# The second mixer's attention, run one head pair behind itself

## The chip, the cores and the metric

One core of a Trainium2 chip runs the whole program. The metric is the time of one execution in device microseconds. TensorE (PE in the profile, PEld for its weight loads), VectorE (DVE), ScalarE (ACT), GpSimd (POOL) and SyncE (SP) each work through a queue of their own, in order, and wait for one another at semaphores.

## What is computed

Two groups of tokens (512 and 256, width 1024) go through the same two-layer encoder trunk. Each layer is a half-weighted SwiGLU block, a mixer, and another such block. The change lies in the mixer of the second layer, an attention of 16 heads of 64 in which each token sees a neighbourhood on a grid 64 wide, with a bias by relative position:

```python
def neighbourhood_attn(q, k, v, rpb):
    ...
    def one_row(args):
        ...
        bias = rpb[:, dr][:, :, dc]
        s = jnp.einsum('bchd,bacjhd->bhcaj', q_row, k_win).astype(jnp.float32) * (HEAD_DIM ** -0.5)
        s = s + jnp.transpose(bias, (0, 2, 1, 3)).astype(jnp.float32)[None]
        p = jax.nn.softmax(s.reshape(B, NA_HEADS, GRID_W, kh * NA_KW), axis=-1)
        p = p.reshape(B, NA_HEADS, GRID_W, kh, NA_KW).astype(v.dtype)
        return jnp.einsum('bhcaj,bacjhd->bchd', p, v_win)

def mixer_c(h, w_qkv, rpb, w_out):
    qkv = (h @ w_qkv).reshape(B, L, 3, NA_HEADS, HEAD_DIM)
    o = neighbourhood_attn(qkv[:, :, 0], qkv[:, :, 1], qkv[:, :, 2], rpb)
    return o @ w_out
```

## The kernel before

Activations lie transposed, with the width over the partitions. Every product of 32-bit numbers is done as three matmuls of a high and a low part (`hi*hi + hi*lo + lo*hi`), so each operand is first split: ScalarE rounds the high part (lines 111 and 193), VectorE subtracts it (112 and 194).

`mixer1` makes queries and keys for one pair of heads at a time (`qk`), and values for four heads at a time (`v_heads`). These projections are the steady work of TensorE; they write `ps_mm`. Beside them runs the attention, a Python generator. `mm3` counts an estimated time for every matmul, and `tick` resumes a generator when this clock has passed the gap that it yielded (`GAPS1`). So the order of TensorE's queue is fixed when the program is built; the other queues are ordered by the compiler's scheduler. A generator that waits for a list to fill yields 0.5 until it is full.

The steps of one head pair `pr`:

- `scores`: three portions `s` of two blocks for both heads, 12 matmuls each into two banks of the pool `aux` (four PSUM banks, used in turn). `finish_rows` then takes, on VectorE, bias and minimum (line 878), on ScalarE the exponential with its sum (883), on VectorE the reciprocal (890) and the scaling of four sets of rows (892). The result lies in the tiles `p{parity}{block}{head}`, two sets by the parity of `pr`.
- `turn`: four transposes on TensorE (line 141) into one `aux` bank, split into `th` and `tl`. Three of them for each head.
- `values_a`, `values_b`: value matmuls of one head into two `aux` banks, which `put` adds up into the output `o` (lines 1255 and 1256).

Before, a pair's three portions come first, then the transposes and values of its first head, then those of the second. The next pair's bias is made on GpSimd (1172) from tables that SyncE loads (1165). `parts` writes the queries and keys of a pair when the pair ahead has been scored.

`mixer_out` is the output projection. It begins with the chunks of six pairs (`early`): each output is split into `oh` and `ol`, the projections go on while the last attention runs, and line 826 adds the old activations.

Of the kernel before, what the change touches and what calls it, by code (L numbers as in the profile page):

```python
# [10 lines left out]
F32R = mybir.dt.float32r  # L11
# [5 lines left out]
P = 128  # L17
D = 1024
KD = D // P
FF = 2816  # L20
NPAIR = FF // (2 * P)
TA, TB = 512, 256
T = TA + TB
# [20 lines left out]
WTOTAL = 12 * D * FF + 8 * EARLY * P * D + D * 1792 + 2 * D * D + D * 3072 + D * 512  # L44
GAP0 = 4.6
SGU = (8.0, 3.0, 4.0)
GAPS1 = (2.4, 3.0, 0.7, 2.0, 0.8)


class Trunk:  # L50
# [1096 lines left out]
    def mixer1(self):  # L1147
        nc = self.nc
        mp = self.mixer_open("m1")
# [11 lines left out]
        def bias(h):  # L1161
            ba = mp.tile([P, 8, 32], F32, tag="ba", name="ba", bufs=2)
            bb = mp.tile([P, 4, 48], F32, tag="bb", name="bb", bufs=2)
            for t, tab in zip((ba, bb), self.tabs):
                nc.sync.dma_start(t.rearrange("p a c -> p (a c)"), tab[h])
            ba, bb = ba.rearrange("p a c -> p c a"), bb.rearrange("p a c -> p c a")
            res, o = [], 0
            for src, k0, k1 in ((ba, 8, 32), (ba, 0, 32), (ba, 0, 24), (bb, 8, 48), (bb, 0, 40)):
                n = (k1 - k0) * src.shape[2]
                a = mp.tile([P, n], F32, tag=f"add{len(res)}", name="add", bufs=2)  # L1170
                v = lambda t: t.rearrange("p (c a) -> p c a", c=k1 - k0)
                nc.gpsimd.tensor_tensor(out=v(a), in0=v(mb[:, o : o + n]), in1=src[:, k0:k1, :], op=ALU.subtract)
                o += n
                res.append(a)
            return res
# [6 lines left out]
        for par in (0, 1):  # L1182
            for j, (_, c0, c1, s0) in enumerate(SCORE):
                for h in (0, 1):
                    t = pp[par, j, h] = mp.tile([P, 256], F32, tag=f"p{par}{j}{h}", name=f"p{par}{j}{h}")
# [5 lines left out]
        def scores(pr, s):  # L1191
            q, k, st = heads[pr][:3]
            ps = [self.psum(self.aux, "aux") for _ in (0, 1)]
            ps_list, outs, sums = [], [], []
            for i in (0, 1):
                j = 2 * s + i
                qc, c0, c1, s0 = SCORE[j]
                n = c1 - c0
                o = i * (160 if s == 2 else 256)
                dst = [t[:, o : o + n] for t in ps]  # L1200
                rows = lambda h: slice(h * 64, h * 64 + 64)
                self.halves3(
                    dst, [tuple(t[rows(h), qc : qc + P] for t in q) for h in (0, 1)],
                    [tuple(t[rows(h), c0:c1] for t in k) for h in (0, 1)],
                )
                ps_list += dst
                outs += [pp[pr % 2, j, h][:, s0 : s0 + n] for h in (0, 1)]
                sums += [adds[2 * pr + h][(0, 1, 1, 2, 3, 4)[j]] for h in (0, 1)]
            self.finish_rows(mp, st, 4 * s, ps_list, outs, sums, [3e38] * 4)

        def split_t(src):
            pt = self.psum(self.aux, "aux")
            for i, s in enumerate(src):
                self.tpose(pt[:, i * P : (i + 1) * P], s)
            th = mp.tile([P, 512], F32R, tag="th", name="th", bufs=4)
            tl = mp.tile([P, 512], F32R, tag="tl", name="tl", bufs=4)
            self.split(th, tl, pt)
            return th, tl

# [7 lines left out]
        def turn(pr, t, h):  # L1227
            return split_t([pp[pr % 2, j, h][:, c] for j, c in TURN[t]])

        def values_a(po, vt, hv, ii, tt):  # L1230
            for i in (2 * ii, 2 * ii + 1):
                c = (i % 2) * 256
                for t in tt:
                    if i == 0:
                        dst = po.rearrange("p (j q) -> p j q", j=4)[:, 0::3, :]
                        rhs = t[:, c : c + 256].rearrange("p (j q) -> p j q", j=2)
                    else:
                        dst = po[:, (i - 1) * P : (i + 1) * P]
                        rhs = t[:, c : c + 256]
                    self.mmul(  # L1240
                        dst, vt[i][:, hv, :], rhs, i == 0 and t is tt[0], i == 3 and t is tt[1], skip_group_check=True
                    )

        def values_b(po, vt, hv, tt):
            for b in range(2):
                for t in tt:
                    self.mmul(
                        po[:, 0:256], vt[4 + b][:, hv, :], t[:, b * 256 : b * 256 + 256],
                        b == 0 and t is tt[0], b == 1 and t is tt[1],
                    )  # L1250

        def put(pr, h, po, c0, c1):
            n = c1 - c0
            tb = mp.tile([P, 512], F32, tag="tb", name="tb")[0:64, :n]
            nc.scalar.copy(tb, po[64:128, :n])
            nc.vector.tensor_tensor(
                out=ot[pr][h * 64 : h * 64 + 64, c0:c1], in0=po[0:64, :n], in1=tb, op=ALU.add
            )

        heads, scored, adds = [], [], {}  # L1260

        def attention():
            for pr in range(8):
                while pr >= len(heads):
                    yield 0.5
                q, k, st, vt, hv = heads[pr]
                for s in range(3):
                    scores(pr, s)
                    if s < 2:
                        yield GAPS1[0]  # L1270
                scored.append(pr)
                for h in (0, 1):
                    adds.pop(2 * pr + h)
                    if 2 * pr + h + 2 < 16:
                        adds[2 * pr + h + 2] = bias(2 * pr + h + 2)
                yield GAPS1[1]
                tt = {}
                for h in (0, 1):
                    for t in range(3):
                        tt[t, h] = turn(pr, t, h)  # L1280
                        yield GAPS1[2]
                    while len(vt) < 6:
                        yield 0.5
                    yield GAPS1[3]
                    po = self.psum(self.aux, "aux")
                    for t in (0, 1):
                        values_a(po, vt, hv + h, t, tt[t, h])
                        yield GAPS1[4]
                    put(pr, h, po, 0, TA)
                    po = self.psum(self.aux, "aux")  # L1290
                    values_b(po, vt, hv + h, tt[2, h])
                    put(pr, h, po, TA, T)
                    yield GAPS1[4]

        adds[0], adds[1] = bias(0), bias(1)
        att = self.spawn(attention())
        def parts(pr, t, vt, hv):

# [26 lines left out]
        def v_heads(qd, vt):  # L1325
            wv = sum((self.unit("l1_w_qkv", 4 * i, 4, 2048 + qd * 256, 256) for i in (0, 1)), [])
            for i in range(6):
                ps = self.psum()
                for k in range(KD):
                    self.mm3(  # L1330
                        ps[:, 0:256], self.xcols(k, i * P, (i + 1) * P), wv[k],
                        k == 0, k == KD - 1,
                    )
                pv = ps[:, 0:256].rearrange("p (h d) -> p h d", h=4)
                v = mp.tile([P, 4, P], F32R, tag="vt", name="vt", bufs=9)
                r = self.ry[:, i : i + 1]
                nc.scalar.activation(v[:, :, 0:64], pv, AF.Copy, scale=r)
                nc.vector.scalar_tensor_tensor(
                    out=v[:, :, 64:128], in0=pv, scalar=r, in1=v[:, :, 0:64].bitcast(F32),
                    op0=ALU.mult, op1=ALU.subtract,  # L1340
                )
                vt.append(v)

        last = None
        for qd in range(4):
            for i in (0, 1):
                if last:
                    self.drain(last)
                new = qk(2 * qd + i)
                if i == 0:  # L1350
                    vt = []
                last = self.spawn(parts(2 * qd + i, new, vt, 2 * i))
                if i == 0:
                    v_heads(qd, vt)
        self.drain(last)
        self.mixer_out("l1_w_out", [ot[k] for k in range(KD)], att, True)


# [182 lines left out]
```

## Time and profile before

| | |
|---|---|
| median of 3 runs | 2680.07 us (2679.75 to 2681.55) |
| profiled execution | 2677.91 us, span 2676.1 us |
| mean granted clock of TensorE | 0.988 |
| second mixer, scores of pair 0 to values of pair 7 | about 1809 to 2104 us of the span |
| TensorE busy from 1860 to 2060 | 36.4 to 38.6 us of each 40 |

Lines of the profile name engine, source line, operation and tiles (out<-in). A wait is idle time of an engine just before an instruction, put down to what released it. Matmuls overlap: one of 0.28 us may start 0.11 us after the one before it. The gap between starts tells more than the busy time.

### The profile page before, as it was taken

Reading aid. Unit: us, or ns where it says so; the run is one execution under the profiler, and the core shown is the slowest. Engines: PE = TensorE matmul, PEld = TensorE weight load, DVE = VectorE, ACT = ScalarE, POOL = GpSimd, SP = SyncE. Lnnn points to the kernel's source line nnn. Section 1 sums busy time; section 2 is a strip of 40 time slices with the busy share of each in tenths; the row PEclk is TensorE's granted clock in tenths of the full one; section 3 lists DMA queues with packets and bytes.
Section 4 is the critical chain, followed back from the end, with each engine's and each line's share of the span. In section 5 each row is a group of like instructions: output and inputs, shape, how many; then the busy total and the mean of one; then the engine's idle time right before and its main releaser. Section 6 shows DMA issues by size and latency. Waiting matters only on the chain.

```text
span 2676.1 us, 41168 instructions
## 1 busy us (share of the span) xinstructions
PE 2583.9 (97%) x15150; PEld 2510.0 (94%) x15150; DVE 2263.4 (85%) x4748; ACT 1372.1 (51%) x2847; POOL 80.5 (3%) x124
## 2 busy tenths in 40 slices
PE   6999999999999999999999999999999989999997
PEld 6999999977889999999999999988888989999997
DVE  8988889789769988898998898886666599888886
ACT  7545444555756544455654454454545365454443
POOL 0000000000100000000000000011111100000000
PEclk9999999999999999999999999989999999999999
DMA  5333222421223222222322222232211322222221
GB/s 164 116 86 98 78 65 72 148 72 38 86 75 91 79 68 79 64 79 79 95 79 71 72 74 69 79 116 62 62 55 43 99 87 79 79 64 79 65 86 55
DMA packets 82746, 214.80 MB, mean 80 GB/s; under 512 B 19952, under 2 KB 32752, under 8 KB 82544
## 3 DMA queue, kind: packets, MB, share of 16 engines
q1 hardware_dynamic: 82400, 212.14, 25.8%
q8 instruction: 119, 1.95, 0.3%
q14 instruction: 83, 0.68, 0.1%
q10 hardware_dynamic: 144, 0.03, 0.0%
HBM read 202.70 MB, written 15.07 MB: 81 GB/s over the span
## 4 chain that ended last, share of the span: by engine, by line
PE 88%; DVE 6%; ACT 4%; issue 1%; DMA 0%; SPq 0%; DVEq 0%; ACTq 0%
PE ps_mm L137 56%; PE ps_aux L137 31%; ACT p L883 2%; DVE p L892 1%; PE ps_aux L141 1%; DVE wlo L112 1%; DVE xl L710 1%; ACT whi L111 0%; DVE p L878 0%; DMA raw<-in_w 0%; ACT xh L709 0%; DVE x L632 0%; DVE x L677 0%; DVE ol L194 0%; ACT sq L216 0%
## 5 line engine op out<-in xcount | busy, mean ns | idle before, releaser
L111 ACT CAST whi<-s 128x512 fp32r<-128x512 f32 x496 | 302.0, 620 | 377.6 <-DVE s L580 134.1
L111 ACT CAST whi<-raw 128x512 fp32r<-128x512 f32 x512 | 311.7, 618 | 283.6 <-PE ps_mm L137 127.8
L112 DVE TENSOR_TENSOR wlo<-s,whi 128x512 fp32r<-128x512 f32 x496 | 335.0, 685 | 71.6 <-ACT whi L111 71.2
L112 DVE TENSOR_TENSOR wlo<-raw,whi 128x512 fp32r<-128x512 f32 x494 | 335.8, 685 | 39.1 <-ACT whi L111 34.5
L137 PE MATMUL ps_aux<-dt,whi 128*128 128x384 f32 x864 | 221.6, 338 | 0.0
L137 PE MATMUL ps_mm<-db,whi 128*128 128x384 f32 x864 | 221.6, 338 | 0.0
L137 PEld LDWEIGHTS ps_mm<-db,whi 128*128 128x128 f32 x864 | 156.8, 188 | 0.0
L137 PEld LDWEIGHTS ps_aux<-dt,whi 128*128 128x128 f32 x864 | 156.8, 188 | 0.0
L137 PE MATMUL ps_mm<-xh,whi 128*128 128x512 f32 (+1 forms) x416 | 147.7, 355 | 3.0 <-ACT xh L709 3.0
L137 PE MATMUL ps_mm<-db,wlo 128*128 128x384 f32 x432 | 146.0, 338 | 0.0
L137 PE MATMUL ps_aux<-dt,wlo 128*128 128x384 f32 x432 | 146.0, 338 | 0.0
L137 PE MATMUL ps_mm<-xl,whi 128*128 128x512 f32 (+1 forms) x416 | 142.7, 343 | 1.1 <-DVE xl L710 1.1
L137 PE MATMUL ps_mm<-xh,wlo 128*128 128x512 f32 (+1 forms) x416 | 142.2, 342 | 0.0
L472 DVE TENSOR_TENSOR u<-ps_aux,u 128x384 f32<-128x384 f32 x176 | 96.9, 551 | 5.2 <-PE ps_aux L137 3.9
L580 DVE TENSOR_TENSOR s<-raw,raw 128x512 f32<-128x512 f32 x124 | 83.3, 685 | 20.8 <-DMA raw<-in_w 20.8
L467 ACT COPY u<-ps_mm 128x384 f32<-128x384 f32 x176 | 83.5, 474 | 33.4 <-PE ps_mm L137 33.2
L137 PE MATMUL ps_aux<-dh,whi 128*128 128x384 f32 x384 | 98.5, 338 | 0.6 <-DVE x L677 0.6
L580 DVE TENSOR_TENSOR s<-raw 128x512 f32<-128x512 f32 x124 | 84.8, 685 | 16.8 <-DMA raw<-in_w 16.8
L883 ACT ACTIVATE p<-p,st 128x256 f32<-128x256 f32 (+3 forms) x144 | 69.2, 481 | 54.2 <-DVE st L878 54.1
L632 DVE TENSOR_TENSOR x<-ps_aux,x 128x384 f32<-128x384 f32 x160 | 86.3, 551 | 11.1 <-PE ps_aux L137 11.0
L137 PE MATMUL ps_mm<-oh,whi 128*128 128x384 f32 x256 | 89.6, 350 | 5.1 <-DVE x L861 4.0
L632 DVE TENSOR_TENSOR x<-ps_mm,x 128x384 f32<-128x384 f32 x160 | 86.8, 550 | 6.1 <-PE ps_mm L137 5.9
(427 smaller groups left out, 8087.2 us busy)
## 6 DMA issues: line engine op xcount, KB each, us to landing
raw<-in_w SPq DMA_DIRECT2D x342, 512.0 KB, 3.7
xdm<-x SPq DMA_DIRECT2D x16, 384.0 KB, 2.4
x<-in_x SPq DMA_DIRECT2D x16, 192.0 KB, 5.6
x<-xdm SPq DMA_DIRECT2D x8, 384.0 KB, 3.5
xold<-xdm SPq DMA_DIRECT2D x8, 384.0 KB, 3.1
out_y<-y SPq DMA_DIRECT2D x8, 384.0 KB, 2.5
tab<-skew SPq DMA_DIRECT2D x8, 256.0 KB, 4.4
raw<-in_w SPq DMA_DIRECT2D x8, 256.0 KB, 2.6
```

The lines of the kernel that those rows point to most:

```text
L111: nc.scalar.copy(hi, src)
L112: (eng or nc.gpsimd).tensor_tensor(out=lo, in0=src, in1=hi.bitcast(F32), op=ALU.subtract)
L137: self.nc.tensor.matmul(out, lhsT=lhsT, rhs=rhs, start=start, stop=stop, **kw)
L141: self.nc.tensor.transpose(out, src, self.ident)
L467: nc.scalar.copy(e[n, out], bank[key, n])
L472: nc.vector.tensor_tensor(out=t, in0=bank[key, n], in1=t, op=ALU.add)
L580: f = lambda o, x, y, op: self.nc.vector.tensor_tensor(out=o, in0=x, in1=y, op=op)
L632: nc.vector.tensor_tensor(out=o, in0=ps, in1=o, op=ALU.add)
L710: nc.vector.scalar_tensor_tensor(out=lo, in0=src, scalar=gain, in1=hi.bitcast(F32), op0=ALU.mult, op1=ALU.subtract)
L883: nc.scalar.activation(outs[i - n0], outs[i - n0], AF.Exp, scale=-1.0, bias=mn[:, i : i + 1], accum_out=sm[:, i : i + 1])
L892: nc.vector.tensor_scalar(out=outs[i - n0], in0=outs[i - n0], scalar1=ri[:, i : i + 1], scalar2=None, op0=ALU.mult)
```

## The change

The generator now keeps the pair before as `old`. In each cycle the three portions of the new pair alternate with the old pair's work: portion 0, transposes of the first head, portion 1, values of the first head, portion 2, then transposes and values of the second head. A ninth cycle has the last pair's transposes and values alone. Rings of tiles change with it: `th` and `tl` 4 to 3 each, `vt` 9 to 12. The gaps are set anew, and the output projection begins when six pairs have their values.

```diff
-GAPS1 = (2.4, 3.0, 0.7, 2.0, 0.8)
+GAPS1 = (2.4, 0.9, 2.0, 0.7, 1.6)
...
-            th = mp.tile([P, 512], F32R, tag="th", name="th", bufs=4)
-            tl = mp.tile([P, 512], F32R, tag="tl", name="tl", bufs=4)
+            th = mp.tile([P, 512], F32R, tag="th", name="th", bufs=3)
+            tl = mp.tile([P, 512], F32R, tag="tl", name="tl", bufs=3)
...
+        def turned(pr, vt, hv, h):
+            tt = []
+            for t in range(3):
+                tt.append(turn(pr, t, h))
+                yield GAPS1[1] if t < 2 else GAPS1[2]
+            while len(vt) < 6:
+                yield 0.5
+            return tt
+
+        def valued(pr, vt, hv, h, tt):
+            po = self.psum(self.aux, "aux")
+            for t in (0, 1):
+                values_a(po, vt, hv + h, t, tt[t])
+                yield GAPS1[3]
+            put(pr, h, po, 0, TA)
+            po = self.psum(self.aux, "aux")
+            values_b(po, vt, hv + h, tt[2])
+            put(pr, h, po, TA, T)
+            yield GAPS1[4]
...
+            old = None
+            for pr in range(9):
+                new = None
+                while pr < 8 and pr >= len(heads):
+                    yield 0.5
+                if pr < 8:
+                    new = pr, *heads[pr][3:]
+                    scores(pr, 0)
+                    yield GAPS1[0]
+                if old:
+                    tt = yield from turned(*old, 0)
+                if new:
+                    scores(pr, 1)
+                    yield GAPS1[0]
+                if old:
+                    yield from valued(*old, 0, tt)
+                if new:
+                    scores(pr, 2)
+                    scored.append(pr)
...
+                    yield GAPS1[0]
+                if old:
+                    tt = yield from turned(*old, 1)
+                    yield from valued(*old, 1, tt)
+                    done.append(old[0])
+                old = new
...
-                v = mp.tile([P, 4, P], F32R, tag="vt", name="vt", bufs=9)
+                v = mp.tile([P, 4, P], F32R, tag="vt", name="vt", bufs=12)
...
         self.drain(last)
+        self.run_until(lambda: len(done) >= KD - 2)
         self.mixer_out("l1_w_out", [ot[k] for k in range(KD)], att, True)
```

Each queue holds the same instructions as before. Where they stand, at three places (digits at the end of a name are buffer numbers):

TensorE, pair 3, before: from the last matmul of its third portion of scores (`kh`, `ql`) to the first transpose. Its operand `p100` is a row tile of parity 1, of pair 3 itself.

```order
L137 MATMUL ps_aux1476_21101<-kh_20999,ql_20998 128x160
L137 MATMUL ps_mm1470_21030<-xh5_18912,whi1467_21016 128x512
L137 MATMUL ps_mm1470_21030<-xl5_18920,whi1467_21016 128x512
L137 MATMUL ps_mm1470_21030<-xh5_18912,wlo1467_21017 128x512
L137 MATMUL ps_mm1470_21030<-xh6_18913,whi1467_21016 128x512
L137 MATMUL ps_mm1470_21030<-xl6_18921,whi1467_21016 128x512
L137 MATMUL ps_mm1470_21030<-xh6_18913,wlo1467_21017 128x512
L137 MATMUL ps_mm1470_21030<-xh7_18914,whi1467_21016 128x512
L137 MATMUL ps_mm1470_21030<-xl7_18922,whi1467_21016 128x512
L137 MATMUL ps_mm1470_21030<-xh7_18914,wlo1467_21017 128x512
L141 MATMUL ps_aux1477_21164<-ident_80,p100_19342 128x128
```

The same engine with the change: from the last matmul of pair 3's first portion to the next transpose.

```order
L137 MATMUL ps_aux1462_20941<-kh_20905,ql_20904 128x256
L137 MATMUL ps_mm1460_20936<-xh1_18908,whi1456_20918 128x512
L137 MATMUL ps_mm1460_20936<-xl1_18916,whi1456_20918 128x512
L137 MATMUL ps_mm1460_20936<-xh1_18908,wlo1456_20919 128x512
L137 MATMUL ps_mm1460_20936<-xh2_18909,whi1456_20918 128x512
L137 MATMUL ps_mm1460_20936<-xl2_18917,whi1456_20918 128x512
L137 MATMUL ps_mm1460_20936<-xh2_18909,wlo1456_20919 128x512
L141 MATMUL ps_aux1463_20973<-ident_80,p000_19322 128x128
```

The transposes behind pair 3's first portion now read `p000`, of parity 0: those of pair 2.

VectorE, pair 3, before: from the reciprocal of the third portion to the last split of the first head's transposes (`tl`), among it work on the next queries (`qk`, `ql`).

```order
L890 RECIPROCAL st_21883<-st_21883 128x4
L1320 TENSOR_TENSOR qk0_22055<-ps_mm1528_21912,rt_19465 128x512
L892 TENSOR_SCALAR p140_19354<-p140_19354,st_21883 128x160
L892 TENSOR_SCALAR p141_19356<-p141_19356,st_21883 128x160
L892 TENSOR_SCALAR p150_19358<-p150_19358,st_21883 128x160
L892 TENSOR_SCALAR p151_19360<-p151_19360,st_21883 128x160
L194 TENSOR_TENSOR tl_22052<-ps_aux1535_22046,th_22051 128x512
L1322 COPY qk0_22055<-qk0_22055 128x64
L194 TENSOR_TENSOR tl_22068<-ps_aux1537_22062,th_22067 128x512
L910 SCALAR_TENSOR_TENSOR ql_22240<-qk0_22055,qh_22239 128x576
L194 TENSOR_TENSOR tl_22080<-ps_aux1538_22074,th_22079 128x512
```

With the change: from the instruction behind the third portion's last minimum to the last split of the second head's transposes of pair 2.

```order
L910 SCALAR_TENSOR_TENSOR ql_21275<-qk0_21042,qh_21274 128x576
L1338 TENSOR_TENSOR qk0_21154<-ps_mm1468_21045,rt_19465 128x512
L890 RECIPROCAL st_20907<-st_20907 128x4
L1340 COPY qk0_21154<-qk0_21154 128x64
L892 TENSOR_SCALAR p140_19354<-p140_19354,st_20907 128x160
L892 TENSOR_SCALAR p141_19356<-p141_19356,st_20907 128x160
L892 TENSOR_SCALAR p150_19358<-p150_19358,st_20907 128x160
L892 TENSOR_SCALAR p151_19360<-p151_19360,st_20907 128x160
L194 TENSOR_TENSOR tl_21151<-ps_aux1473_21145,th_21150 128x512
L194 TENSOR_TENSOR tl_21170<-ps_aux1475_21164,th_21169 128x512
L112 TENSOR_TENSOR wlo1481_21256<-raw258_21249,whi1481_21255 128x512
L194 TENSOR_TENSOR tl_21185<-ps_aux1476_21179,th_21184 128x512
```

The splits `tl` of another pair's transposes, and a weight's split (`wlo`), now stand behind the reciprocal and the scaling of pair 3's third portion; `ql` and the scaling of `qk` moved ahead of that reciprocal.

VectorE at the stage's end, pair 7, before: around the reciprocal of its first portion, with `ol6` a split for the output projection.

```order
L112 TENSOR_TENSOR wlo1603_23082<-raw271_23079,whi1603_23081 128x512
L194 TENSOR_TENSOR ol6_22788<-o6_22238,oh6_22780 128x384
L890 RECIPROCAL st_22765<-st_22765 128x4
L878 ISA p120_19348,st_22765<-ps_aux1587_22872,add_22393 128x256
L878 ISA st_22765 128x1
L892 TENSOR_SCALAR p100_19342<-p100_19342,st_22765 128x192
L892 TENSOR_SCALAR p101_19344<-p101_19344,st_22765 128x192
L892 TENSOR_SCALAR p110_19346<-p110_19346,st_22765 128x256
L892 TENSOR_SCALAR p111_19347<-p111_19347,st_22765 128x256
```

With the change: the same reciprocal and what follows it.

```order
L112 TENSOR_TENSOR wlo1593_22988<-raw271_22985,whi1593_22987 128x512
L826 TENSOR_TENSOR x0_22700<-ps_mm1574_22738,xold_22811 128x384
L890 RECIPROCAL st_22671<-st_22671 128x4
L892 TENSOR_SCALAR p100_19342<-p100_19342,st_22671 128x192
L892 TENSOR_SCALAR p101_19344<-p101_19344,st_22671 128x192
L892 TENSOR_SCALAR p110_19346<-p110_19346,st_22671 128x256
L892 TENSOR_SCALAR p111_19347<-p111_19347,st_22671 128x256
L194 TENSOR_TENSOR tl_22784<-ps_aux1577_22778,th_22783 128x512
L194 TENSOR_TENSOR tl_22796<-ps_aux1578_22790,th_22795 128x512
L194 TENSOR_TENSOR tl_22808<-ps_aux1579_22802,th_22807 128x512
```

Where the second portion's minima stood between the reciprocals, there now stand line 826's addition ahead and the splits of pair 6's transposes behind.

More of the change, by code (lines that the diff above doesn't have):

```diff
@@ L1258, in put @@
             )
-        heads, scored, adds = [], [], {}
+        heads, scored, done, adds = [], [], [], {}
+        def turned(pr, vt, hv, h):
[16 more added lines that the diff above has]
+            yield GAPS1[4]
@@ L1262, in attention @@
         def attention():
-            for pr in range(8):
-                while pr >= len(heads):
+            old = None
+            for pr in range(9):
+                new = None
+                while pr < 8 and pr >= len(heads):
                     yield 0.5
[L1266 to L1293, printed above, removed]
@@ new lines, in attention @@
+                if pr < 8:
[12 more added lines that the diff above has]
+                    scored.append(pr)
+                    for h in (0, 1):
+                        adds.pop(2 * pr + h)
+                        if 2 * pr + h + 2 < 16:
+                            adds[2 * pr + h + 2] = bias(2 * pr + h + 2)
+                    yield GAPS1[0]
```

## The prediction

> **What bounds the kernel now.** I read the page's busy shares and chain first, then the table of stretches, the list of waits over the second mixer, and last the timeline of one pair and of the stage's end.
>
> ```profile
> span 2676.1 us, 41168 instructions
> PE 2583.9 (97%) x15150; PEld 2510.0 (94%) x15150; DVE 2263.4 (85%) x4748; ACT 1372.1 (51%) x2847; POOL 80.5 (3%) x124
> PE 88%; DVE 6%; ACT 4%; issue 1%; DMA 0%; SPq 0%; DVEq 0%; ACTq 0%
> ```
>
> TensorE carries 88% of the chain that ended last, so the time falls only where TensorE stands still or runs slowly. For the second mixer that place is the list of waits from 1790 to 2140 us (columns: total us, times, longest):
>
> ```profile
> PEld ps_aux L141 <- DVE p L892: 19.2, 20, 2.3
> PE ps_aux L141 <- DVE p L892: 15.4, 18, 2.1
> PEld ps_aux L141 <- POOL add L1172: 2.1, 2, 1.2
> DVE st L890 <- ACT p L883: 23.9, 22, 1.1
> PEld ps_mm L137 <- DVE ol L194: 0.8, 1, 0.8
> ```
>
> Nearly all of TensorE's waiting here is one thing: the transposes (L141) wait for the normalised scores (L892). VectorE itself waits 1.1 us a portion for ScalarE's exponentials (L890). Pair 3 shows the chain:
>
> ```profile
> 1927.38 0.28 PE L137 MATMUL ps_aux<-kh,ql 64*128 64x256 f32 x2
> 1927.80 0.36 DVE L878 CUSTOM_DVE_ANT_0 p<-ps_aux,add 128x192 f32<-128x192 f32 x1
> 1929.69 0.49 ACT L883 ACTIVATE p<-p,st 128x256 f32<-128x256 f32 x1
> 1930.52 1.07 DVE L892 TENSOR_SCALAR p<-p,st 128x192 f32<-128x192 f32 x4
> 1934.68 0.27 PE L141 MATMUL ps_aux<-ident,p 128*128 128x128 f32 x1
> 1935.49 0.55 PE L141 MATMUL ps_aux<-ident,p 128*128 128x128 f32 x3 [0.54 <-DVE p L892]
> 1935.59 0.31 DVE L878 CUSTOM_DVE_ANT_0 p<-ps_aux,add 128x160 f32<-128x160 f32 x1
> 1936.59 0.60 PE L141 MATMUL ps_aux<-ident,p 128*128 128x128 f32 x4
> 1938.40 0.93 DVE L892 TENSOR_SCALAR p<-p,st 128x160 f32<-128x160 f32 x4
> 1938.75 0.97 PE L141 MATMUL ps_aux<-ident,p 128*128 128x128 f32 x4 [0.86 <-DVE p L892]
> ```
>
> From the first portion's last score (about 1927.6) to its last normalised row (1931.59) pass 4.0 us. Four transposes issue in 0.45 us when nothing holds them: the group at 1936.59 takes 0.60 with 0.27 of latency, so 0.11 us each. The first group loses 1935.49 - 1934.68 - 0.11 = 0.70 us. The third follows the second by 0.45 us and three 512-column matmuls of about 0.23 us, thus was due at 1937.73, began 1.02 us late, and took 0.37 us too long. Pair 3 loses 2.1 us.
>
> The stage's end costs more, and there the clock falls too (columns: start:end, length, busy us of PE, PEld, DVE, ACT and POOL with instructions, granted clock, DMA share, GB/s):
>
> ```profile
> 2081.40:2084.80 3.40, 1.29 (x9) 0.90 (x8) 3.37 (x16) 1.70 (x7) 0.00 (x0) 1.00 0.01 4
> 2084.80:2091.60 6.80, 5.84 (x22) 5.20 (x21) 5.12 (x14) 3.62 (x12) 1.30 (x1) 0.50 0.29 74
> ```
> ```profile
> 1937.00:1940.00 3.00, 2.05 (x11) 1.31 (x10) 2.27 (x9) 1.77 (x6) 1.19 (x3) 1.00 0.24 66
> ```
>
> A stretch with TensorE busy 1.29 of 3.40 us is followed by 6.8 us at half clock; pair 3, busy 2.05 of 3.00 us, keeps the full clock.
>
> **The change, part by part.** No engine gains or loses work; it is order alone.
>
> (1) A pair's transposes now read scores normalised a whole portion cycle earlier. Every L141 wait on L892 should go. PE's row (15.4 us) counts too little, because each of its 18 waits is hidden behind about 0.17 us of matmul latency (0.28 us long, 0.11 us apart): 18.5 us. PEld's two rows give 21.3 us. Seven pairs like pair 3 and a last one of 3.6 us (below) would give 18.3. I take 20, ends 15.4 and 21.3.
>
> (2) The half-clock stretch followed the 2.3 us wait of pair 7's transposes. Without that wait I expect full clock: 5.84 busy us would take half, 2.9 us less; the stretch holds a further wait already counted, so I take 2.5, ends 0 and 2.9.
>
> (3) New joints. Between two portions the four PSUM banks of the attention pool now go round scores (2), transposes (3), values (2), so scores and values wait for the splits of the transposes, which stand on VectorE behind the portion's own reciprocal. The prices:
>
> ```profile
> L194 DVE TENSOR_TENSOR tl<-ps_aux,th 128x512 fp32r<-128x512 f32 x42 | 28.0, 683 | 0.4
> L1256 DVE TENSOR_TENSOR o<-ps_aux,tb 64x512 f32<-64x512 f32 x14 | 9.6, 684 | 17.7 <-ACT tb L1255 17.6
> L910 DVE SCALAR_TENSOR_TENSOR ql<-qk,qh 128x576 fp32r<-128x576 f32 x7 | 5.3, 758 | 1.3 <-ACT qh L909 1.3
> L1338 DVE SCALAR_TENSOR_TENSOR vt<-ps_mm,sm,vt 128x256 fp32r<-128x256 f32 x23 | 11.0, 477 | 17.0 <-ACT vt L1337 17.0
> ```
> ```profile
> 1861.04 0.40 PE L137 MATMUL ps_mm<-xh,wlo 128*128 128x512 f32 x1
> 1861.27 0.40 PE L137 MATMUL ps_mm<-xh,whi 128*128 128x512 f32 x1
> ```
>
> The two matmuls of 512 columns start 0.23 us apart; 256 and 384 columns are taken as a half and three quarters of that.
>
> Joint a, odd pairs, second portion's scores: their second bank is free when the first transposes are split, 4.0 + 0.68 = 4.7 us after the first portion's scores. In the new order 21 projections of 0.23 us and 12 transposes, 6.2 us, stand between. Slack 1.5 us. Joint b, odd pairs, the second head's last values: from the third portion's first minimum (1935.59) to its last normalised row (1939.33) 3.74 us, then 0.76 (ql now in between), three splits of 0.68 and one weight split of the same size: 7.2 us. Between them stand six projections of 0.23, 33 of 0.12 (256 columns: half of 512), 12 transposes and 8 value matmuls of 0.12: 7.6 us. Slack 0.4 us, the thinnest. Even pairs have about the same cover, and on VectorE one value split of 0.48 (vt) in place of ql, the weight split and the scaling of qk: slack about 2 us. A joint can only wait, so the lower end is 0; I allow 1.0 us for all joints before the end, upper end 7 (1 us a pair).
>
> (4) The end. Before and after, the splits of the six finished outputs (ol) stand on VectorE ahead of pair 7's scores:
>
> ```profile
> 2074.25 2.89 DVE L194 TENSOR_TENSOR ol<-o,oh 128x384 fp32r<-128x384 f32 x6
> 2077.06 0.34 DVE L878 CUSTOM_DVE_ANT_0 p<-ps_aux,add 128x192 f32<-128x192 f32 x1
> 2079.86 1.07 DVE L892 TENSOR_SCALAR p<-p,st 128x192 f32<-128x192 f32 x4
> 2081.61 0.33 PE L141 MATMUL ps_aux<-ident,p 128*128 128x128 f32 x1
> 2081.75 0.80 DVE L826 TENSOR_TENSOR x<-ps_mm,xold 128x384 f32<-128x384 f32 x1
> 2084.04 0.55 PE L141 MATMUL ps_aux<-ident,p 128*128 128x128 f32 x3 [2.11 <-DVE p L892]
> 2088.29 0.90 PE L141 MATMUL ps_aux<-ident,p 128*128 128x128 f32 x3 [0.96 <-DVE p L892]
> ```
>
> Pair 7's old waits are 2084.04 - 2081.61 - 0.11 = 2.3 and about 1.3 us, the 3.6 of term 1. Now pair 6's transposes stand there, whose data are old. What is late next: the output projection reaches chunk 4 before ol of it is done (2074.25 + 3 x 0.48 = 2075.7): 0.4 us, and 0.1 at chunk 5. The third transposes need the first scores' bank, read by VectorE's third minimum operation about 1.0 us after 2077.06: 0.9 us. The next scores need the first split: minima done 2078.4, then a weight split 0.68, L826 0.80, reciprocal 0.2, rows 1.07, tl 0.68, so 2081.8, against TensorE's 2078.0 + 0.45 + 12 x 0.17 = 2080.5: 1.2 us. Together 2.6 us, ends 0 and 5. The 0.8 us on ol stays.
>
> [...]
>
> (5) Things moved at no cost. The new wait for six finished pairs ahead of the output projection: pair 5's last values stand 108 matmuls before pair 7's first scores, so nothing is queued behind it. The th/tl rings shrink to three, and a head issues three; the next head's first write follows the previous head's values, a score portion earlier. On SyncE the bias loads keep their place, but wait for GpSimd's adds, which wait for portions now spread out. Behind them stand the weight loads:
>
> ```profile
> 1937.69 0.85 SPq L1165 DMA_DIRECT2D bb<-tab  x2
> 1948.05 4.49 SPq L96 DMA_DIRECT2D raw<-in_w  x2
> ```
>
> The third portion moves from about 5 to 13.7 us after the first, so bb would issue near 1946.5; the weights behind it went at 1948.05. Hidden, with 1.5 us to spare, and what is loaded there has a whole value stage until it is multiplied. The splits of the weights on VectorE now lie between attention work. TensorE's list shows no wait on them before, so I price them at nothing; one split of 0.68 us late at each of seven changes of weights would cost 4.8 us, inside the range's upper end.
>
> Sum: -20 - 2.5 + 1.0 + 2.6 = -18.9 us. The profiled execution took 2677.9 us (span 2676.1 and 1.8 around it), 2.2 under the runs' median of 2680.1. On the median: 2661.2 us.
>
> **The rivals.**
>
> Waits come back in part: joints a and b lose 1 us a pair (7 instead of 1.0) and the half clock stays (+2.5). For it: slack of 0.4 us in joint b, and VectorE's scaling of four rows, 0.93 and 1.07 us above, took 1.48 while GpSimd's adds of the bias ran:
>
> ```profile
> 1932.08 2.98 POOL L1172 TENSOR_TENSOR add<-mb,ba 128x256 f32<-128x256 bf16 x4 [2.54 <-DVE st L878]
> 1934.19 1.48 DVE L892 TENSOR_SCALAR p<-p,st 128x256 f32<-128x256 f32 x4
> ```
>
> -18.9 + 6 + 2.5 = -10.4: 2669.7 us.
>
> Waits merely move: splits instead of normalised rows are what TensorE waits for, about 20 us in all, which needs 0.6 us at each of five joints in seven pairs. Against it: the slack worked out. 2680 us, within the 0.2% (5.4 us) that a measurement can tell.
>
> Slower, by VectorE's queue: each portion's splits stand behind its reciprocal, which waits for ScalarE. If a joint is late by 0.9 us, 35 joints cost 31 us against 22.5 saved: 2689 us. It decides from 0.65 us a joint; the thinnest joint would have to miss by that beyond its 0.4, the others by far more.
>
> Slower, by the clock: if every burst of 12 transposes let the clock fall for 3.4 us, 14 bursts at 1.7 us cost 24 us: net +5, 2685 us. The row 1937:1940, with as many transposes and full clock, speaks against it. [...]
>
> That the change does not do what it says is ruled out by the order of instructions.
>
> **How the numbers follow.** Forecast as summed: 0.70, its own range 2656 (21.3 + 2.9 saved, nothing new) to 2667 (half of joint loss). Partial: 0.15. Same: 0.07. Slower: 0.05 by the queue, 0.03 by the clock. So faster by over 0.2% 0.85, same 0.07, slower 0.08. The range reaches from 2655.5 to 2672, past the partial case.
>
> **What would show it.** L141's waits on L892 vanish from TensorE's list; if they stay, term 1 is wrong. New small waits of L141 and L137 on tl or L878 near 2075-2082 us show term 4; a granted clock of 1.00 there shows term 2. Waits of ps_aux L137 on tl in each pair mean the partial rival. PEld waiting on wlo would mean that the weights' splits, squeezed between attention work on VectorE, are late, the term at nothing that could prove me wrong most.

## The result, and the profile after

The changed kernel takes 2660.37 us, median of four runs (2657.44 to 2661.16); the kernel before took 2679.91 us beside it (2678.62 to 2681.55, four runs). The ratio is 0.9927 as the two medians stand, 0.9925 over the runs with a 95% interval of 0.9913 to 0.9937: 20 us faster. Forecast were 2661.2 us and a range of 2655.5 to 2672. The profiled execution has a span of 2659.4 us against 2676.1.

The page of the changed kernel, the same three lines as before (span; busy time of each engine; the chain that ended last):

```profile
span 2659.4 us, 41163 instructions
PE 2582.3 (97%) x15150; PEld 2513.1 (94%) x15150; DVE 2262.8 (85%) x4748; ACT 1371.3 (52%) x2847; POOL 82.7 (3%) x124
PE 91%; DVE 5%; ACT 3%; DMA 0%; issue 0%; SPq 0%; DVEq 0%; ACTq 0%
```

The work is the same to about 3 us on each engine. The chain now has 91% of TensorE where it had 88%. What went is waiting, and the list of waits from 1790 to 2140 us shows which (total us, times, longest):

```profile
DVE st L890 <- ACT p L883: 21.1, 20, 1.1
...
PEld ps_mm L137 <- DVE x L861: 2.6, 2, 2.1
...
PE ps_mm L137 <- DVE x L861: 2.0, 2, 1.8
...
PEld ps_aux L141 <- DVE st L878: 1.0, 1, 1.0
...
PE ps_aux L141 <- DVE st L878: 0.7, 1, 0.7
...
PE ps_aux L137 <- DVE tl L194: 0.5, 1, 0.5
...
PE ps_mm L137 <- DVE ol L194: 0.5, 1, 0.5
```

No row has L141 waiting on L892 any more. VectorE's own wait for the exponentials is still there, 20 times and 1.1 us at the longest: the chain of scores, minimum, exponential and scaling takes about as long as before (here from 1932.25, the end of the last scores' matmul, to 1936.43, 4.2 us), but the transposes no longer stand behind it. Pair 3's third portion shows it:

```profile
1931.98 0.27 PE L137 MATMUL ps_aux<-kh,ql 64*128 64x160 f32 x2
1932.39 0.32 DVE L878 CUSTOM_DVE_ANT_0 p<-ps_aux,add 128x160 f32<-128x160 f32 x1 [1.04 <-PE ps_aux L137]
1933.68 0.60 PE L141 MATMUL ps_aux<-ident,p 128*128 128x128 f32 x4
1934.83 0.60 PE L141 MATMUL ps_aux<-ident,p 128*128 128x128 f32 x4
1935.50 0.93 DVE L892 TENSOR_SCALAR p<-p,st 128x160 f32<-128x160 f32 x4
1935.98 0.60 PE L141 MATMUL ps_aux<-ident,p 128*128 128x128 f32 x4
```

The transposes follow the scores by 1.7 us and each group takes 0.60 us, the length of a group that nothing holds. They run ahead of and beside this portion's scaling (1935.50), since they read the pair before.

The stage's length says more than the span, since the two profiled executions also differ elsewhere. From pair 0's first scores to the last matmul of the output projection it is 347.1 us before and 326.7 after: 20.4 us less, both taken from the start of the first matmul and of the last. The spans differ by 16.7 only: 3.8 us had been lost ahead of this stage in the execution after, which had two stretches of half clock (near 880 and 1375 us) that the one before did not have. The medians carry no such accident.

The end of the stage, where new waits were forecast (columns as above; in brackets the idle time and what ended it):

```profile
2056.03 0.44 PE L137 MATMUL ps_mm<-ol,whi 128*128 128x384 f32 x1 [0.48 <-DVE ol L194]
2059.27 0.66 PE L141 MATMUL ps_aux<-ident,p 128*128 128x128 f32 x4 [0.70 <-DVE st L878]
2060.09 0.84 DVE L826 TENSOR_TENSOR x<-ps_mm,xold 128x384 f32<-128x384 f32 x1
2061.05 1.07 DVE L892 TENSOR_SCALAR p<-p,st 128x192 f32<-128x192 f32 x4
2062.04 1.28 DVE L194 TENSOR_TENSOR tl<-ps_aux,th 128x512 fp32r<-128x512 f32 x2
2062.87 0.35 PE L137 MATMUL ps_aux<-kh,qh 64*128 64x256 f32 x1 [0.54 <-DVE tl L194]
```

Both new waits are there and are named as forecast: pair 6's third transposes wait for pair 7's minimum operation (L878), its next scores for the first split (tl) behind line 826 and the scaling. Measured from start to start of the matmuls (the distance between two starts, less the distance that such matmuls keep when nothing holds them) they cost 0.86 and 0.81 us.

A table of stretches (columns as in the prediction: start:end, length, busy us of five engines, granted clock, DMA share, GB/s) shows pair 3, the end of the attention, and two neighbouring stretches of 3.41 us in the output projection behind it:

```profile
1937.00:1940.00 3.00, 3.00 (x28) 3.00 (x27) 3.00 (x7) 2.07 (x5) 0.00 (x0) 1.00 0.29 41
2058.00:2064.00 6.00, 4.76 (x34) 3.93 (x33) 5.97 (x20) 3.94 (x12) 2.73 (x2) 1.00 0.23 66
2129.43:2132.84 3.41, 1.64 (x9) 1.32 (x9) 3.41 (x8) 1.98 (x5) 0.00 (x0) 1.00 0.00 0
2132.84:2136.25 3.41, 3.41 (x13) 3.41 (x12) 2.14 (x5) 1.40 (x3) 0.00 (x0) 0.50 0.02 5
```

The half clock at pair 7's transposes is gone. A new one of 3.41 us stands at 2132.84, behind a wait for VectorE's additions at line 861, which both kernels have. A matmul of 384 columns takes 0.32 us there instead of 0.17, so the stretch costs 1.6 us. It was not forecast; what goes with it is told at the end.

### The profile page after: what moved, and what is told of

Read it like the earlier page. It is cut to its first block, busy times and chain, and to the rows that moved or that the text cites. A ratio compares the mean times of both kernels' runs of the same rounds, so it can differ in the third digit from the quotient of the medians.

```text
span 2659.4 us, 41163 instructions
## 1 busy us (share of the span) xinstructions
PE 2582.3 (97%) x15150; PEld 2513.1 (94%) x15150; DVE 2262.8 (85%) x4748; ACT 1371.3 (52%) x2847; POOL 82.7 (3%) x124
## 3 DMA queue, kind: packets, MB, share of 16 engines
q8 instruction: 119, 1.95, 0.3%
## 4 chain that ended last, share of the span: by engine, by line
PE 91%; DVE 5%; ACT 3%; DMA 0%; issue 0%; SPq 0%; DVEq 0%; ACTq 0%
PE ps_mm L137 59%; PE ps_aux L137 32%; PE ps_aux L141 1%; DVE wlo L112 1%; DVE xl L710 1%; ACT whi L111 0%; DMA raw<-in_w 0%; ACT xh L709 0%; DVE x L677 0%; DVE ol L194 0%; ACT sq L216 0%; DVE x L632 0%; ACT p L883 0%; ACT diag L247 0%; DVE tmp L348 0%
## 5 line engine op out<-in xcount | busy, mean ns | idle before, releaser
L137 PEld LDWEIGHTS ps_mm<-xh,whi 128*128 128x128 f32 x416 | 79.4, 191 | 14.2 <-ACT xh L709 4.1
```

The costliest lines, as they stand in the source:

```text
L137: self.nc.tensor.matmul(out, lhsT=lhsT, rhs=rhs, start=start, stop=stop, **kw)
```

## The experiments

**Theory.** TensorE waited because a portion's transposes came sooner after its scores than VectorE and ScalarE can normalise. An order that puts 4.0 us or more in between frees the 20 us, as long as VectorE comes to the scores at once. In the new order the splits of the transposes take the place of the scaling as what could be late; they have a small slack. **Rivals:** the gain comes from the lag of a pair itself (VectorE's work spread more evenly); or VectorE's queue sets the pace, so that every microsecond on it is paid.

**The changed kernel again**, on the chip of the next three runs, to have both kernels beside them.

> The changed kernel once more, beside the others on the same chip. Both theories: 0.9925 of the kernel before (0.9913 to 0.9937 as measured).

2658.74 us (2656.18 to 2661.37), ratio 0.9921 (0.9909 to 0.9933), the kernel before 2680.43. The stage took 326.6 us in its profile, as in the first.

**No normalising, before and after.** The second mixer's reciprocal and scaling are left out of both kernels, so that its output isn't normalised; TensorE's order is that of each kernel.

```diff
-    def finish_rows(self, pool, st, n0, ps_list, outs, adds, init, sink=None):
+    def finish_rows(self, pool, st, n0, ps_list, outs, adds, init, sink=None, scaled=True):
...
+        if not scaled:
+            return
         nc.vector.reciprocal(ri[:, n0:n], sm[:, n0:n])
...
-            self.finish_rows(mp, st, 4 * s, ps_list, outs, sums, [3e38] * 4)
+            self.finish_rows(mp, st, 4 * s, ps_list, outs, sums, [3e38] * 4, scaled=False)
```

> The kernel before, with the reciprocal and the scaling of the scores (lines 890 and 892) left out in the second mixer: the output is not normalised there. The transposes then wait for the exponentials alone, a chain about 1.3 us shorter a portion (0.18 + 1.07). Theory A (the gain of the change is this chain, taken out of TensorE's way): the L141 waits fall from about 20 us to 3 to 8, and the time falls by 13 to 18 us, to about 0.994. Rival B (the gain comes from where TensorE's matmuls stand, or from the rings, whatever the chain): the time stays within 4 us of the kernel before.

2654.9 us, the median of three runs, ratio 0.9908 (0.9894 to 0.9922); a fourth run took 6530 us, for a reason that nothing here shows, and is not counted. Without the scaling the old order loses nothing either. TensorE's list of waits, whole, from 1790 to 2140 us:

```profile
PE ps_mm L137 <- DVE x L861: 2.0, 2, 1.8
PE ps_aux L137 <- ACT diag L247: 1.1, 1, 1.1
PE ps_mm L137 <- DVE ol L194: 0.5, 1, 0.5
PE ps_aux L141 <- ACT p L883: 0.2, 1, 0.2
```

More went than the 13 to 18 us expected: I had counted on transposes that still wait for the exponentials, and that is 0.2 us once. The stage took 323.5 us, 23.6 less than before: some 20 us of waits, and most of the rest for the 6.8 us of half clock, of which this stage has none.

> The changed kernel with lines 890 and 892 left out in the second mixer in the same way. Theory A: the chain is already covered, so at most the 1.7 us of small waits at the stage's end go; 0 to 3 us below the changed kernel. Rival B: it loses as much as the kernel before does by the same edit; if VectorE's load mattered (34 us of scaling and reciprocals gone), 5 us or more.

2657.73 us, ratio 0.9918 (0.9906 to 0.993), stage 325.8 us: within 0.9 us of the changed kernel's stage, and the wait on tl at the end (0.81 us) is what went. With the change, the scaling costs nothing on the path, apart from that wait.

**The old order with other gaps.** The kernel before, one line changed: portions 3.6 apart instead of 2.4, and 5.5 instead of 3.0 ahead of the transposes; the later gaps are shortened. No lag, no new order of parts.

```diff
-GAPS1 = (2.4, 3.0, 0.7, 2.0, 0.8)
+GAPS1 = (3.6, 5.5, 0.4, 1.0, 0.5)
```

> The kernel before with other gaps alone, GAPS1 = (3.6, 5.5, 0.4, 1.0, 0.5): no pair runs behind itself, but the portions stand 24 projections (even pairs) or 12 (odd) apart, and 4.9 us of projections, not 2.1, stand ahead of the first transpose, taken from the room between transposes and values. Theory A in its plain form (only the distance between normalising and transposing counts): the L141 waits fall to under 5 us and the time to 2660 to 2666. Rival C (there is no room for both in one pair's cycle without the lag): values and transposes of the second head wait for splits instead, 1 to 2 us a pair, and the time is 2670 to 2680.

2658.54 us (2655.12 to 2660.01), ratio 0.9919 (0.9907 to 0.993); stage 324.3 us. Same gain, to within what can be measured. Of the 21.3 us on PEld and the 15.4 us on PE that L141 waited on L892, this is left (from PEld's list; PE's has no such row):

```profile
PEld ps_aux L141 <- DVE p L892: 0.6, 2, 0.3
```

So the lag is one way to keep transposes clear of the scaling, not the only one, and the rival that the lag itself pays falls. So does the thought that the new rings of tiles pay, since this kernel has the old ones.

**One number.** Of those five gaps only the second is changed, 3.0 to 5.5.

```diff
-GAPS1 = (2.4, 3.0, 0.7, 2.0, 0.8)
+GAPS1 = (2.4, 5.5, 0.7, 2.0, 0.8)
```

> The kernel before with one number changed: the gap between a pair's last score portion and its first transpose, 3.0 to 5.5; portions, transposes and values keep their spacing. Theory A (all that cost time was the distance from a portion's scaling to its transposes): the first transposes come 4.9 us after the last scores and the third 7.2 us after them, both beyond the 4.0 us that normalising takes, so L141 no longer waits on L892 and about 20 us go: 2659 us. Rival B (the spacing of the portions matters too, since VectorE normalises the third portion late): half of the waits stay, on the third transposes, 2669 us. Rival C (the lag of one pair is what pays): no gain, 2680 us.

2659.49 us (2657.19 to 2662.33), ratio 0.9924 (0.9911 to 0.9938); the kernel before 2678.43 beside it. From pair 0 to pair 6 no matmul starts 0.2 us late. Only pair 7 still loses 0.91 and 1.33 us from start to start, and half clock follows for 3.4 us. Its third transposes come 7.8 us after its last scores, and that is not enough, since VectorE is behind: six splits `ol` of the output projection stand ahead of its first minimum, and it reaches the third portion's minima at 2071.50, 5.1 us after the last of their scores began (2066.39). One row of the scaling is stretched as well:

```profile
2061.57 2.89 DVE L194 TENSOR_TENSOR ol<-o,oh 128x384 fp32r<-128x384 f32 x6
2071.50 0.32 DVE L878 CUSTOM_DVE_ANT_0 p<-ps_aux,add 128x160 f32<-128x160 f32 x1
2072.36 0.60 PE L141 MATMUL ps_aux<-ident,p 128*128 128x128 f32 x4
2073.87 1.95 DVE L892 TENSOR_SCALAR p<-p,st 128x160 f32<-128x160 f32 x4
2074.21 1.30 POOL L112 TENSOR_TENSOR wlo<-raw,whi 128x512 fp32r<-128x512 f32 x1 [8.59 <-DVE p L892]
2074.23 0.33 PE L141 MATMUL ps_aux<-ident,p 128*128 128x128 f32 x1 [0.74 <-DVE p L892]
2075.66 0.90 PE L141 MATMUL ps_aux<-ident,p 128*128 128x128 f32 x3 [1.11 <-DVE p L892]
```

The scaling took 1.95 us here, with a subtraction of GpSimd beside it, where four such rows took 0.93 above: one of the four took 1.31. Nearly the whole gain of the change is thus worth one number: the distance from a pair's last scores to its first transposes.

**How thin the new joints are: gaps halved.** The changed kernel with all five gaps halved.

```diff
-GAPS1 = (2.4, 0.9, 2.0, 0.7, 1.6)
+GAPS1 = (1.2, 0.45, 1.0, 0.35, 0.8)
```

> The changed kernel with its five gaps halved (1.2, 0.45, 1.0, 0.35, 0.8): the attention of a pair is bunched, and then waits for the next queries and keys. Theory A (a joint waits for the splits behind its own portion's scaling, and the slack of a joint is the cover on TensorE less the chain on VectorE): joint a of odd pairs has 12 transposes and 12 projections, 4.0 us, for a chain of 4.7, late by 0.7; of even pairs 3.1 us, late by 1.6. Joint b has 6.4 us in odd pairs and 4.9 in even ones for chains of about 7.2 and 6: late by about 1 each. Some 2 us a pair, 14 in all (8 to 25): about 2673 us, with waits of ps_aux matmuls on tl (L194) in every pair. Rival B (the joints had far more slack than worked out, or wait for something else): within 0.2% of the changed kernel, about 2659 us, and no such waits.

2677.38 us (2675.14 to 2682.05), ratio 0.9997 (0.9988 to 1.0006): all of the gain is gone. From start to start, odd pairs lose 1.0 to 1.2 us and even pairs 3.5, 14 us over pairs 1 to 6. That was the forecast sum, but by luck: it had 1.7 us for an odd pair and 2.6 for an even one, and nothing on the additions of the values. The end loses more than was counted (2.8, 1.2 and 1.1 us, and one stretch of half clock more than the changed kernel's profile has), hence 4 us over the forecast. TensorE's list names the splits, the minimum at the end and the additions of the values, and no scaling:

```profile
PE ps_aux L137 <- DVE tl L194: 9.4, 11, 1.0
PE ps_aux L141 <- DVE st L878: 2.6, 1, 2.6
PE ps_aux L141 <- DVE o L1256: 1.7, 3, 0.6
PE ps_aux L137 <- ACT th L193: 1.3, 3, 0.4
```

The same lag with the wrong gaps is thus worth nothing. The rival of the prediction in which waits merely move does happen, with other gaps than the change has.

**How thin the new joints are: more work on VectorE.** In the changed kernel, one or two more passes over each normalised row, in the same order on TensorE.

```diff
-            self.finish_rows(mp, st, 4 * s, ps_list, outs, sums, [3e38] * 4)
+            self.finish_rows(mp, st, 4 * s, ps_list, outs, sums, [3e38] * 4, extra=1)
...
+        for i in list(range(n0, n)) * extra:
+            nc.vector.tensor_scalar(
+                out=outs[i - n0], in0=outs[i - n0], scalar1=1.0, scalar2=None, op0=ALU.mult
+            )
```

> The changed kernel with one more pass on VectorE over each normalised row, a multiplication by 1.0 behind L892 (96 instructions more, about 1 us a portion, 24 us of VectorE in all); TensorE's order is the same. Theory A (slack as worked out: 1.5 us at joint a, 0.4 at joint b of odd pairs, about 2 elsewhere, and here one weight split of 0.68 stands behind the transposes' splits instead of among them): no joint is late, or joint b by a few tenths; only at the stage's end do the scores behind pair 7's first portion wait a further 1.1 us: 2659 + 1 to 3 = about 2661 us. Rival B (VectorE's queue sets the pace, so that each portion's microsecond is paid at a joint): at least 14 us more, 2673 us or above.

2658.05 us (2657.29 to 2658.84), ratio 0.9923 (0.9909 to 0.9936): no slower. No joint from pair 0 to pair 6 is late; at the end the wait on tl grew from 0.81 to 1.55 us, and 3.41 us of half clock followed it (at 2061.50). The stage took 327.4 us, 0.7 more than the changed kernel's: it has no half clock behind L861, so that the clock costs both the same.

> As the run before, with two more passes (192 instructions, about 2 us a portion, 48 us of VectorE). Theory A: joint a of odd pairs 0.6 us late (1.5 - 2.1), joint b 0.8 late (7.2 - 0.68 + 1.9 against 7.6), even pairs just in time, the end 2.2 later: 4 x 1.4 + 2.2 = 8 us, about 2667 us, with waits of ps_aux matmuls on tl in the odd pairs alone. Rival B (VectorE's queue sets the pace): 28 us more or above, 2687 us. Rival C (slack is much larger than worked out): under 3 us more, 2661 us.

2668.37 us (2667.73 to 2671.7), ratio 0.9964 (0.9951 to 0.9976): 10 us slower than with one pass, 8 worked out. TensorE's list has one row for nearly all of it:

```profile
PE ps_aux L137 <- DVE tl L194: 8.4, 7, 2.0
```

That VectorE's queue sets the pace falls with the first of the two: 96 more instructions cost no time that can be measured. But the loss with two passes is not where I had put it. From start to start, odd pairs lose 0.9 us and even pairs 1.6 and 0.2; I had 1.4 for odd pairs and nothing for even ones. Pair 2's third portion, with one extra pass and then with two (L896 is the extra pass; behind one added parameter and the loop, later lines moved by 4):

```profile
1888.01 0.42 DVE L1260 TENSOR_TENSOR o<-ps_aux,tb 64x256 f32<-64x256 f32 x1 [0.49 <-ACT tb L1259]
1889.08 0.31 DVE L878 CUSTOM_DVE_ANT_0 p<-ps_aux,add 128x160 f32<-128x160 f32 x1
1891.21 0.60 PE L141 MATMUL ps_aux<-ident,p 128*128 128x128 f32 x4
1891.61 0.69 DVE L896 TENSOR_SCALAR p<-p 128x160 f32<-128x160 f32 x4
1892.62 1.88 DVE L194 TENSOR_TENSOR tl<-ps_aux,th 128x512 fp32r<-128x512 f32 x3
1893.52 0.28 PE L137 MATMUL ps_aux<-tl,vt 128*128 128x256 f32 x1
```
```profile
1890.06 0.37 ACT L1259 COPY tb<-ps_aux 64x256 f32<-64x256 f32 x1 [3.32 <-DVE o L1260]
1890.46 0.42 DVE L1260 TENSOR_TENSOR o<-ps_aux,tb 64x256 f32<-64x256 f32 x1 [0.49 <-ACT tb L1259]
1891.54 0.31 DVE L878 CUSTOM_DVE_ANT_0 p<-ps_aux,add 128x160 f32<-128x160 f32 x1
1892.54 0.60 PE L141 MATMUL ps_aux<-ident,p 128*128 128x128 f32 x4
1894.07 1.29 DVE L896 TENSOR_SCALAR p<-p 128x160 f32<-128x160 f32 x8
1895.69 1.87 DVE L194 TENSOR_TENSOR tl<-ps_aux,th 128x512 fp32r<-128x512 f32 x3
1896.41 0.39 PE L137 MATMUL ps_aux<-tl,vt 128*128 128x256 f32 x1 [1.40 <-DVE tl L194]
```

A second pass adds 1.29 - 0.69 = 0.60 us to this portion. That is not all: the last minimum stood 2.13 us ahead of the third transposes with one pass (1891.21 - 1889.08) and 1.00 with two, another 1.13 us late, because the additions of the values (L1260) ahead of it on VectorE were late as well. The passes of the second portion hold the first addition back, ScalarE's next copy waits for that addition (3.32 us with two passes), and the second addition, with the minima behind it, waits for the copy. So VectorE's backlog from the second portion ran over into the third. With one pass the first split was done at about 1892.62 + 0.63 = 1893.25 for a matmul at 1893.52, so the slack was 0.27 us; 0.60 + 1.13 - 0.27 = 1.46 against 1.56 measured. The joint that gives way first is the first split ahead of the head's first values, not the third ahead of its last, as the prediction had it. A chain costed within one portion misses what one portion leaves to the next.

## Why the prediction was right, point by point

(1) L141's waits on L892: I took 20 us. In the profile before, summed from start to start, the transposes lost 16.6 us in the pairs before pair 7 and 3.6 in pair 7, 20.2; after, none. The list's 15.4 alone would have been 5 short. The 0.17 us that each wait had hidden behind a matmul's latency are 3 of the 5; the rest are late starts inside a group (0.31 us each, five of them) whose idle time was under 0.1 us and which the list of 18 leaves out. The 20 was chosen between two ends and not worked out, so that it fits so well is partly luck. The runs with other gaps show that the distance is the cause.

(2) The half-clock stretch: 2.5 us, and it went. Besides the wait already counted, the matmuls in the stretch of 6.8 us lost 2.7 us from start to start, and those in the new one of 3.4 us lose 1.6. So the half clock went with the wait, as forecast, and was sized well, and the new stretch behind L861 was missed. The stage's balance has 20.2 + 0.2 (a wait on L878 that went) - 0.86 - 0.81 = 18.7 us of waits and 1.1 us of the clock, 19.8 of the measured 20.4; the 0.6 left are spread over delays of under 0.1 us. The gain on the clock is not safe: with one pass more on VectorE, half clock was back at this place (at 2061.50). That every burst of transposes lets the clock fall, the condition of the rival by the clock, was not seen. The stretch 2058 to 2064, at a granted clock of 1.00, says little on it, since TensorE had little idle time there (busy 4.76 of 6.00 us). The profile before says more: from 1965.31 to 1968.73 us TensorE was idle for 1.87 us and had 0.90 us of transposes, and the granted clock was 1.00 there and in the 3.41 us that followed.

(3) The new joints: 1.0 us, measured 0 (no matmul of pairs 0 to 6 starts 0.15 us late). This is the term that was mis-sized, on the safe side. Its slack was thin all the same, as the run with two passes shows (10 us).

(4) The end: 2.6 us, measured 1.7. The transposes on L878 lost 0.86 (0.9), the scores on tl 0.81 (1.2); the 0.4 and 0.1 on ol at the later chunks did not appear, since two groups of transposes (2056.48 and 2057.45) stand ahead of chunk 4 and the wait on L878 ahead of chunk 5: TensorE took chunk 4 at 2058.06, when its split had been done for 1.2 us. The 0.8 us on ol stayed, 0.64 from start to start.

(5) At nothing: no row of TensorE's list in this stage has it waiting for a weight's low part (wlo) or for a table's load. That the smaller rings of th and tl cost nothing is read from that list alone; the new order wasn't tried with the old rings.

The sum, -18.9, had 1.0 us too much in (3) and 0.9 in (4), and some tenths too little in (1) and (2); the new half clock of 1.6 us goes the other way. These errors partly cancel, so that a total within 1 us of the measured time owes something to luck. The upper end 2667 of the forecast's own range is 2661.2 plus the whole joint loss of term 3 beyond 1.0 us, not half of it. The rivals: no partial return, no new wait in each pair, no clock drop between 1815 and 2130 us; the queue rival was wrong by the run with one more pass, though with halved gaps or two passes its mechanism is there.

## What to carry to other kernels

Where one engine waits for another's chain at a fixed place in its order, work out the chain (here 4.0 us from scores to scaled rows) and the cover (the work that stands between the two places on the waiting engine) before rebuilding the order: here one number, a gap of 5.5 for 3.0, gave what a lag of one pair gave. A new order has its own joints; those with some tenths of slack hold only as long as the queue behind them carries no backlog from portion to portion, and extra passes on the suspected engine, one and then two, show how much slack there is. Sum waits from start to start of the waiting engine's instructions: where they overlap, the list of waits leaves out what the latency hides (here 4.8 of 20.2 us).

## What the runs showed of the hardware

In the profiles before and after, half clock (a granted clock of 0.50) comes in stretches of 3.41, 6.83 or 13.65 us, but for the last one, of 13.1 us, which runs to the program's end. In each of the two the starts of these stretches lie whole multiples of 3.413 us apart: before, 599.98 and 2084.78 by 435 of them; after, 1375.09 and 2132.84 by 222. Reckoned from the first instruction, the first stretch starts at 26.54 us in the one profile and at 26.82 in the other. An interval is here what lies between two neighbouring places of such a raster.

The wait on L861 near the end of the output projection is 1.94 us from start to start before, after and with one extra pass, and its place in the raster went with what followed. After the change, and with one extra pass:

```profile
2132.24 0.45 PE L137 MATMUL ps_mm<-oh,whi 128*128 128x384 f32 x1 [1.77 <-DVE x L861]
```
```profile
2131.34 0.44 PE L137 MATMUL ps_mm<-oh,whi 128*128 128x384 f32 x1 [1.77 <-DVE x L861]
```

In the first the wait lies whole in the interval 2129.43 to 2132.84, and half clock follows; in the second the boundary at 2129.77 (20 times 3.413 us behind the half clock at 2061.50) cuts it into 0.36 and 1.57 us, and none follows. In the profile before, where the wait ends at 2150.47, the boundary at 2149.63 cuts it into 1.10 and 0.84 us, and none follows. Over the 184 intervals at full clock between 1815 and 2135 us of the profiles before and after, the two that half clock followed had TensorE idle for 2.6 us (before, from 2081.37) and 2.0 (after, from 2129.43), reckoned from the starts of its matmuls; of all others only two had more than 1.9 (2.1 and 2.0, before, from 1818.54 and 2036.99), and in these 0.8 us of the rest were transposes. So half clock followed two of the four intervals with that much idle time, and whether the wait on L861 cost 1.6 us more went with its place in the raster. Part of the spread between runs may come from this; no run separates it.

VectorE's scaling of four rows took 0.93 us, and 1.95 with a subtraction of GpSimd beside it. Row by row this is one held instruction: three of the four took 0.29 to 0.30 us, and the one that began at 2074.30, behind the start of GpSimd's at 2074.21, took 1.31 and ended 0.1 us after GpSimd's. The profile before has one such row too, from 2086.93, behind GpSimd's start at 2086.83: 1.31 us. In the profile before, six rows of 128x256 that lay wholly beside a GpSimd instruction took 0.35 us, as those without one did, so running side by side is not by itself slow. This was seen at places of the traces and not tested by a run of its own, and what decides which row is held stays open.
